# A batched matrix product whose engines run on hand-written semaphores, with one buffer of transposes, one of rounded y and three of x

## The chip, the cores and the metric

The kernel runs on one core of a Trainium2 chip. The metric is the device time of one execution in microseconds (us): 134.47 us before the change, the median of three executions (134.36 to 134.61). The profile covers one execution, from its first instruction to its last, which is a little shorter than the device time: its span is 132.9 us.

Five engines take part. TensorE (PE in the profile) multiplies, VectorE (DVE) and ScalarE (ACT) copy and convert, SyncE (SP) only issues DMA transfers, which sixteen DMA engines then carry out. GpSimd (POOL) does nothing but set up four constants.

## The reference

```python
batch, dim_i, dim_j, dim_k = 32, 256, 512, 384
# x: (32, 256, 512) float32, y: (32, 512, 384) float32
np.einsum('bij,bjk->bik', x, y).astype(np.float32)
```

So there are 32 independent products of a 256 x 512 and a 512 x 384 matrix. Both kernels round x and y to 16-bit floating point for the multiplication and accumulate in 32 bits.

## The kernel before

The batch is worked off in N = 8 iterations of four matrices each (Q = 4). Each of the four occupies 32 of the 128 partitions. An iteration n consists of these parts, and letters stand for them:

- x, y: the loads of 2.1 MB of x and 3.1 MB of y, both issued by SyncE.
- T: VectorE rounds x to 16 bits (one cast, 128 x 4096) and transposes it in two halves, e = 0 and e = 1.
- R: VectorE rounds y to 16 bits in four casts, a quarter each.
- M: TensorE makes 128 products, 64 for each half e. Each uses 32 rows of the array, and four matrices g take turns.
- C and D: ScalarE (C) and VectorE (D) copy the eight PSUM banks, one for each (e, g), into the output tile. A bank is copied in four pieces of 32 partitions, from iteration 6 on in two pieces of 64.
- S: the store of 1.6 MB, issued by SyncE on the same queue as the loads.

The order in which a scheduler keeps them is written down in a plan. Every engine works off its own parts in this order, and the framework places the semaphores from the tiles that the instructions read and write.

```python
PLAN = """
x0 x1 y0
T0 x2 y1
T1 R0 M0 C0 x3 y2
T2 D0 R1 M1 C1 x4 y3
T3 D1 R2 M2 C2 x5 y4
T4 D2 R3 M3 C3 x6 y5
T5 D3 R4 M4 C4 x7 S0 S1 S2 y6
T6 D4 R5 M5 C5 y7
T7 D5 R6 M6 C6 R7 M7 C7 D7 S3 S4 S5 S6 S7
"""
...
    x_pool = ctx.enter_context(tc.tile_pool(name="x_pool", bufs=2))
    y_pool = ctx.enter_context(tc.tile_pool(name="y_pool", bufs=2))
    xr_pool = ctx.enter_context(tc.tile_pool(name="xr_pool", bufs=1))
    xt_pool = ctx.enter_context(tc.tile_pool(name="xt_pool", bufs=3))
    yr_pool = ctx.enter_context(tc.tile_pool(name="yr_pool", bufs=2))
    o_pool = ctx.enter_context(tc.tile_pool(name="o_pool", bufs=O_BUFS))
...
    def on_vector(n, e, g):
        if n < WIDE_GROUPS:                       # WIDE_GROUPS = 6
            return (e, g) == (NE - 1, Q - 1)
        return n == N - 1 and g % 2 == 1
...
    def multiply(n):
        ...
        for e in range(NE):
            for g in range(Q):
                ps_of[n, e, g] = bank[e, g]
            for t in range(T):
                for g in range(Q):
                    s = slice(g * PQ, (g + 1) * PQ)
                    keep(nc.tensor.matmul(ps_of[n, e, g], xt[s, e, t // 2, :, t % 2],
                                          y_r[s, t], start=(t == 0), stop=(t == T - 1)))
```

So half e of M needs four PSUM banks at once, which C and D of the iteration before must have emptied; there is one set of eight banks.

## Time and profile before

| what | before |
|---|---|
| device time | 134.47 us (134.36 to 134.61) |
| span of the profiled execution | 132.9 us |
| mean granted TensorE clock | 0.848 |
| busy: PE, VectorE, ScalarE | 61.5, 96.1, 91.7 us |
| moved by DMA | 54.68 MB, mean 412 GB/s |
| HBM read, written | 41.94 MB, 12.58 MB |
| one cast of x | 2.29 us (8 of them) |
| one transpose, 128 x 1024, and 128 x 512 | 2.00 us (12), 1.08 us (8) |
| one cast of a quarter of y | 0.953 us (32) |
| one copy out of PSUM, ScalarE and VectorE | 0.471 us (192), 0.556 us (32) |
| SyncE's waits before y loads, for VectorE's cast of y | 29.8 us |
| SyncE's waits before stores, for ScalarE's copies | 24.4 us |

How to read it: busy time is how long an engine executed instructions; a wait is put down to whatever ended it. The slices in the profile cut the span into 40 equal pieces of 3.3 us each, and a digit is the busy share in tenths. Where lines of a timeline are shown, the first two numbers are start and length in us, and the bracket at the end tells how long the engine sat idle before the first of these instructions and what released it. L followed by a number is a line of the kernel; a q behind an engine's name stands for its sequencer, which for SyncE is the one that issues DMA. The landing of a transfer is when its last part is reported as complete.

### The profile page before, as it was taken

Reading aid. Unit: us, or ns where it says so; the run is one execution under the profiler, and the core shown is the slowest. Engines: PE = TensorE matmul, PEld = TensorE weight load, DVE = VectorE, ACT = ScalarE, POOL = GpSimd, SP = SyncE. Lnnn points to the kernel's source line nnn. Section 1 sums busy time; section 2 is a strip of 40 time slices with the busy share of each in tenths; the row PEclk is TensorE's granted clock in tenths of the full one; section 3 lists DMA queues with packets and bytes.
Section 4 is the critical chain, followed back from the end, with each engine's and each line's share of the span. In section 5 each row is a group of like instructions: output and inputs, shape, how many; then the busy total and the mean of one; then the engine's idle time right before and its main releaser. Section 6 shows DMA issues by size and latency. Waiting matters only on the chain.

```text
span 132.9 us, 2437 instructions
## 1 busy us (share of the span) xinstructions
PE 61.5 (46%) x1024; PEld 34.9 (26%) x1024; DVE 96.1 (72%) x92; ACT 91.7 (69%) x193; POOL 0.2 (0%) x4
## 2 busy tenths in 40 slices
PE   0000004990399129924952395329540079887100
PEld 0000002550147014612541153115320034455000
DVE  0049999699959999999997999699951090735600
ACT  3000000089999999999999999999999961998500
POOL 0000000000000000000000000000000000000000
PEclk9999999999658975797799869985999555999955
DMA  4999999999999999999999999999999999999993
GB/s 109 429 424 441 451 414 429 446 429 412 419 471 407 404 437 441 432 409 446 429 417 414 456 432 402 414 419 429 429 464 429 414 451 400 419 425 412 400 412 141
DMA packets 3723, 54.68 MB, mean 412 GB/s; under 512 B 384, under 2 KB 384, under 8 KB 896
## 3 DMA queue, kind: packets, MB, share of 16 engines
q1 hardware_dynamic: 3712, 54.53, 96.9%
q8 instruction: 8, 0.13, 0.4%
q14 instruction: 3, 0.02, 0.0%
HBM read 41.94 MB, written 12.58 MB: 410 GB/s over the span
## 4 chain that ended last, share of the span: by engine, by line
DMA 45%; DVE 19%; ACT 15%; PE 10%; issue 4%; DVEq 1%
DMA x_sb<-in_x_dram 22%; DMA y_sb<-in_y_dram 22%; ACT o_sb L153 15%; PE o_ps L132 10%; DVE xt_sb L113 6%; DVE x_r L106 5%; DVE o_sb L153 4%; DVE y_r L119 4%; DVEq L202 1%; DVEq L106 0%
## 5 line engine op out<-in xcount | busy, mean ns | idle before, releaser
L153 ACT COPY o_sb<-o_ps 32x384 f32<-32x384 f32 (+1 forms) x192 | 90.4, 471 | 32.7 <-PE o_ps L132 25.8
L132 PE MATMUL o_ps<-y_r,xt_sb 32*128 32x384 f16 x1024 | 61.5, 399 | 61.7 <-DVE y_r L119 52.3
L132 PEld LDWEIGHTS <-xt_sb 32*128 32x128 f16 x1024 | 34.9, 113 | 87.9 <-DVE y_r L119 32.8
L119 DVE CAST y_r<-y_sb 128x1536 f16<-128x1536 f32 x32 | 28.5, 953 | 10.3 <-DMA y_sb<-in_y_dram 10.2
L113 DVE STREAM_TRANSPOSE xt_sb<-x_r 128x1024 f32<-128x1024 f32 (+1 forms) x20 | 31.7, 1631 | 0.3
L106 DVE CAST x_r<-x_sb 128x4096 f16<-128x4096 f32 x8 | 18.3, 2292 | 11.1 <-DMA x_sb<-in_x_dram 11.0
L153 DVE COPY o_sb<-o_ps 32x384 f32<-32x384 f32 (+1 forms) x32 | 17.8, 556 | 7.8 <-PE o_ps L132 3.8
L153 ACT ACT_TABLE_LOAD x1 | 1.3, 1283 | 0.7 <-PEq L191 0.7
L191 POOL MEMSET const-uint8-127<- 128x1 uint8 x1 | 0.1, 103 | 0.0
L191 POOL MEMSET const-bfloat16-1.0<- 128x1 bf16 x1 | 0.1, 102 | 0.0
L191 POOL MEMSET const-float32-0.0<- 128x1 f32 x1 | 0.1, 99 | 0.2 <-issue 0.2
L191 POOL MEMSET const-float32-1.0<- 128x1 f32 x1 | 0.1, 99 | 0.0
## 6 DMA issues: line engine op xcount, KB each, us to landing
y_sb<-in_y_dram SPq DMA_DIRECT2D x8, 3072.0 KB, 21.5
x_sb<-in_x_dram SPq DMA_DIRECT2D x8, 2048.0 KB, 22.0
out_dram<-o_sb SPq DMA_DIRECT2D x8, 1536.0 KB, 25.6
```

The costliest lines, as they stand in the source:

```text
L106: keep(nc.vector.tensor_copy(x_r, x_of.pop(n)))
L113: keep(nc.vector.transpose(dst[:, c, e], src[:, c, e]))
L119: keep(nc.vector.tensor_copy(yr_of[n][:, a : a + STEP], y_sb[:, a : a + STEP]))
L132: nc.tensor.matmul(ps_of[n, e, g], xt[s, e, t // 2, :, t % 2], y_r[s, t], start=(t == 0), stop=(t == T - 1),)
L153: keep(copy(o[a : a + w, g // per, h * NE + e], ps[h * w : (h + 1) * w]))
L191: nc = _bacc.Bacc("TRN2", target_bir_lowering=False, num_devices=1)
L202: with _tile.TileContext(nc) as tc:
```

## The change

All engines' instructions are put into one section in which the framework places no semaphore and changes no order. Each engine gets its own list of work, and the kernel allocates and waits on its own semaphores. The purpose is a form in which TensorE's code could be written as a loop over iterations (the switch for that, `LOOP`, is off here, so the products are written out as before). A loop needs its operands at the same addresses in each turn, which is why there is a single buffer of rounded y and a single buffer of transposes for iterations 0 to 6; iteration 7 has a buffer of transposes of its own. The memory that this frees is partly given to a third buffer of x.

The core of the diff (cuts marked by "..."):

```diff
-PLAN = """ ... """
+X_BUFS = 3
+Y_BUFS = 2
+LOOPED = 7
+LOOP = False
+QUEUE = "x0 x1 y0 x2 y1 x3 y2 x4 y3 x5 y4 x6 y5 x7 S0 S1 S2 y6 y7 S3 S4 S5 S6 S7"
+
+VECTOR = """
+X0 T0 R0 X1 T1 R1 X2 D0 T2 R2 X3 D1 T3 R3 X4 D2 T4 R4 X5 D3 T5 R5 X6 D4 T6
+X7 T7 D5 R6 D6 R7 D7
+"""
...
-    x_pool = ... bufs=2      y_pool = ... bufs=2     xr_pool = ... bufs=1
-    xt_pool = ... bufs=3     yr_pool = ... bufs=2    o_pool = ... bufs=O_BUFS
+    x_all = pool.tile([P, X_BUFS, R, J], F32, name="x_sb")
+    y_all = pool.tile([P, Y_BUFS, T, K], F32, name="y_sb")
+    o_all = pool.tile([P, O_BUFS, R, K], F32, name="o_sb")
+    x_r = pool.tile([P, R, J], MM_DT, name="x_r")
+    y_r = pool.tile([P, T, K], MM_DT, name="y_r")
+    xt = [pool.tile([P, NE, TW, P], F32, name=f"xt_sb_{k}") for k in range(2)]
...
     def on_vector(n, e, g):
         if n < WIDE_GROUPS:
             return (e, g) == (NE - 1, Q - 1)
-        return n == N - 1 and g % 2 == 1
+        return g == Q - 1 and e == NE - 1 if n < N - 1 else g % 2 == 1
...
+        def load_x(n):
+            if n >= X_BUFS:
+                eng.wait_ge(x_cast, n - X_BUFS + 1)
+        def load_y(n):
+            if n >= Y_BUFS:
+                eng.wait_ge(y_ready[NA - 1], n - Y_BUFS + 1)
+        def store(n):
+            eng.wait_ge(act_done[NE - 1], n + 2)
+            eng.wait_ge(vec_done, n + 2)
...
+        def transpose_x(n):
+            ...
+            for e in range(NE):
+                if 0 < n < LOOPED:
+                    eng.wait_ge(products, done(n - 1, e, Q - 1))
+                for c in range(b):
+                    i = eng.transpose(dst[:, c, e], src[:, c, e])
+                i.then_inc(x_ready[e], 1)
+        def round_y(n):
+            eng.wait_ge(y_in[n], 16)
+            for a in range(NA):
+                if n > 0:
+                    if a < NA - 1:
+                        eng.wait_ge(y_done, (NA - 1) * (n - 1) + a + 1)
+                    else:
+                        eng.wait_ge(products, done(n - 1, NE - 1, Q - 1))
+                s = slice(a * STEP, (a + 1) * STEP)
+                eng.tensor_copy(y_r[:, s], y_all[:, n % Y_BUFS, s]).then_inc(y_ready[a], 1)
...
+        for e in range(NE):                      # TensorE, one iteration
+            eng.wait_ge(act_done[e], count)
+            if e == NE - 1:
+                eng.wait_ge(vec_done, count)
+            eng.wait_ge(x_ready[e], count)
+            for t in range(T):
+                if e == 0 and t % STEP == 0:
+                    eng.wait_ge(y_ready[t // STEP], count)
+                ... matmul as before, the last of a bank adds 1 to products ...
+                if e == NE - 1 and t % STEP == STEP - 1 and t < T - 1:
+                    i.then_inc(y_done, 1)
...
+    with tc.tile_critical():
+        queue()
+        scalar()
+        vector()
+        tensor()
```

In the string VECTOR, X stands for the cast of x alone and T for the two halves of the transpose; the other letters are as above. VectorE works it off from left to right. Iteration 6's bank (1, 3) is now VectorE's to copy (D6), so ScalarE has two copies fewer.

## The prediction

> **What bounds the kernel now.** I read the 40 slices first, then the DMA queues, then each engine in order of time.

> ```profile
> DVE  0049999699959999999997999699951090735600
> ACT  3000000089999999999999999999999961998500
> PEclk9999999999658975797799869985999555999955
> DMA  4999999999999999999999999999999999999993
> q1 hardware_dynamic: 3712, 54.53, 96.9%
> ```

> Only the DMA row is full from the second slice to the last but one: the one queue works 96.9% of the span. 54.53 MB are moved; the stretches of 4 us between 4 and 124 us show 397 to 451 GB/s. So the kernel is bound by bytes, and the end is set by when the last bytes are queued. That is in the stretches of 1 us near the end (columns: PE, PEld, DVE, ACT, POOL busy, PEclk, DMA share, GB/s) and in the queue's last issue:

> ```profile
> 129.00:130.00 1.00, 0.00 (x0) 0.00 (x0) 0.00 (x0) 0.00 (x0) 0.00 (x0) 0.50 1.03 430
> 130.00:131.00 1.00, 0.00 (x0) 0.00 (x0) 0.00 (x0) 0.00 (x0) 0.00 (x0) 0.50 0.61 252
> ```

> ```profile
> 125.58 0.38 SPq L160 DMA_DIRECT2D out_dram<-o_sb  x1
> ```

> (and, over the eight stores:)

> ```profile
> DMA to landing us min/median/max: 6.5/25.6/31.0
> ```

> The DMA engines run dry at about 130.6 us. The last store S7 is issued at 125.58 and lands after 6.5 us (the minimum of the eight stores), at 132.1; 0.8 us later the span ends. S7 is 1.57 MB, at 420 GB/s 3.7 us of transfer, so S6 in front of it ends at about 130.6 - 3.7 = 126.9. **The slack of S7's issue is therefore about 126.9 - 125.6 = 1.3 us**, less the time a store needs to get going. A change that issues S7 earlier gains almost nothing; one that issues it over a microsecond later pays.

> What leads to S7 is in the timelines of ACT, PE and VectorE (start, us, engine, line, idle before it and its releaser):

> ```profile
> 27.09 81.51 ACT L153 COPY o_sb<-o_ps 32x384 f32<-32x384 f32 x168 [25.08 <-PE o_ps L132]
> 112.60 9.80 ACT L153 COPY o_sb<-o_ps 64x384 f32<-64x384 f32 x20 [4.00 <-issue]
> ```

> ```profile
> 89.25 4.30 PE L132 MATMUL o_ps<-y_r,xt_sb 32*128 32x384 f16 x63 [1.28 <-ACT o_sb L153]
> 95.07 2.78 PE L132 MATMUL o_ps<-y_r,xt_sb 32*128 32x384 f16 x62 [1.52 <-ACT o_sb L153]
> 107.23 8.67 PE L132 MATMUL o_ps<-y_r,xt_sb 32*128 32x384 f16 x131 [9.38 <-DVE y_r L119]
> ```

> ```profile
> 90.10 2.29 DVE L106 CAST x_r<-x_sb 128x4096 f16<-128x4096 f32 x1
> 92.42 4.06 DVE L113 STREAM_TRANSPOSE xt_sb<-x_r 128x512 f32<-128x512 f32 x4
> 97.95 2.26 DVE L153 COPY o_sb<-o_ps 32x384 f32<-32x384 f32 x4 [1.47 <-ACT o_sb L153]
> 106.21 3.56 DVE L119 CAST y_r<-y_sb 128x1536 f16<-128x1536 f32 x4 [5.99 <-DMA y_sb<-in_y_dram]
> 113.71 3.56 DVE L119 CAST y_r<-y_sb 128x1536 f16<-128x1536 f32 x4 [3.94 <-DMA y_sb<-in_y_dram]
> ```

> I write X, T, R, M, C, D for rounding x, transposing, rounding y, products, ScalarE's and VectorE's copies of an iteration, a and b for the two halves (e = 0, 1). **ScalarE is the second limit**: 168 copies (C0 to C5) without a pause, 81.51 / 168 = 0.485 us each, 28 per iteration, 13.59 us. So C_n ends at 27.09 + 13.59 (n + 1): C3 at 81.4, C4 at 95.0 (PE's half b of M5 starts at 95.07, when C4 has freed its banks), C5 at 108.6. VectorE's work per iteration is X 2.29 + T 3.95 + D 2.27 + R 3.57 = 12.1 us, less than that; with two y_r and three xt it runs ahead and has slack at the end: before R6 it waited 5.99 us for y6, before R7 3.94 us for y7.

> [...] M6's first half of 64 took 107.23 to 112.60, 5.4 us (84 ns each), the second about 2.8 us (43 ns); M5's first half, which warmed up on its way, 4.30 us.

> **The change, part by part.**

> 1. *Work.* The same 1024 products, 20 transposes, 40 casts, 24 transfers of the same shapes and nearly the same order; two copies of iteration 6 go from ScalarE to VectorE. Nothing is taken off the DMA engines. Own semaphores replace equally many waits. The section adds a branch in and out and a joint wait; the barriers of before take 0.73 us at the start and 0.8 us at the end, so I allow +0.2 us.

> 2. *Third x buffer.* x2 is issued at about 2 us instead of 10.73. But x0, x1, y0 (7.3 MB) keep the queue busy until about 20 us anyway. Gain 0.

> 3. *R0 before X1.* y0 lands about 20.6 (1.65 plus the shortest y landing, 18.9), and R0 ran at 20.81. M0, and with it the chain of ScalarE, starts 0.2 us earlier.

> 4. *One y_r, one xt for iterations 0 to 6.* T_n's half b must wait for M_(n-1)b, R_n's last quarter for the same, and M_(n-1)b waits for C_(n-2). So VectorE is tied to ScalarE. From C_(n-2)'s end: M_(n-1)b 2.8, T_n b 2.0, R_n 3.6, X 2.3, D 2.3, T_(n+1) a 2.0 = 15.0 us; then T_(n+1) b waits until 13.6 + 2.8 = 16.4. It fits: the period stays 13.59 us, with 1.4 us of slack per turn. ScalarE goes on without pauses, since M_n a starts 7.8 us into C_(n-1) and takes 4.3 to 5.4 of the remaining 5.8 us.
>    The loads: R_n ends at (end of C_(n-2)) + 8.4, R4 at 76.2, R5 at 89.8; before they ended at 76.6 and 90.2. So y6 and y7 are issued as before and the queue stays full.

> 5. *The end, where the tie costs.* T6's half b waits for M5b, which starts with the end of C4 at 95.0 and ends at 97.9. Only then come, in this order, T6b 2.05, X7 2.30, T7 4.07, D5 2.27 and R6, with 0.1 of gaps: 97.9 + 10.8 = **R6 at 108.7 instead of 106.21, +2.5 us**. Before, X7 and T7 ran at 90.10 to 96.5, ahead of M5b. Then:
>    - M6a starts a quarter of R6 (0.95) later, 109.7, and is cold: 4.4 to 5.4 us, to 114.6 (before 112.6); M6b 2.8, to 117.4.
>    - D6 now stands ahead of R7 and waits for all of M6: 2 x 0.56 = 1.1, to 118.7. R7 118.7 to 122.3 (before 113.71 to 117.27): **+5 us**. Of this M7 did not use all: before it was held by C6 on ScalarE, 112.60 + 16 copies, until 120.5 for half b. Now C6 is 14 copies from 114.6, done at 121.4.
>    - M7a ends 0.7 after R7, 123.0; M7b 2.8, 125.8 (before 120.50 + 2.75 = 123.25); D7's last four 2.3, 128.1. **S7 at 128.2 instead of 125.58, +2.6 us.**
>    - S6 is queued at about 121.5, in time. The engines run dry at 126.9, and S7 pays its own start: 128.2 + about 6.2 (a little under the 6.5 of before, which held 1.3 us of queue, but a start of its own: x0 took 8.41 - 0.73 = 7.7 us for 2.1 MB, that is 5.0 of transfer and 2.7 of start and landing; 3.7 + 2.5 = 6.2) = 134.4 instead of 132.1, **+2.3 us**.

> Sum: +2.3 (tail) + 0.2 (section) - 0.2 (R0) = +2.3 us; 134.47 + 2.3 = 136.8.

> **Rivals.** (a) *The transfers hide it all*: DMA is full and bytes are the same, so 134.5 to 135. For it: 96.9%. Against: S7's slack of 1.3 us is smaller than the 2.6 us above; it needs M6a warm early and no wait in D6. (b) *ScalarE starves*: if M_n a takes 5.4 us cold and half b is late each turn, ScalarE pauses every iteration, say 0.5 us over five, so +2.5 more at the tail: 139. For it: the margin is 0.4 us when cold. Against: M3 to M5 took 4.3 us. (c) *The loads run late*, since y_(n+2) waits for R_n which waits for products: the queue would empty near 62 or 75 us. Against: R2 ends at 49 and R3 at 63, 12 us ahead of need. (d) *The third x buffer and less waiting gain*: under 134. Nothing in a full DMA row leaves room; I give it 3 in 100.

> **Range and chances.** The tail's sum has about 1 us of doubt from the clock of M6a and M7a, 0.7 from the start of S7, and rival (a) below and (b) above: 135.0 to 138.8. The 2% line is 137.16, close above my number: slower 0.40, within 0.57, faster 0.03.

> **What would show it.** Right: R6 starts near 108.7 without waiting for DMA; T6's second half is released by PE at about 97.9; R7 is released by VectorE's copies or PE, not by y7; S7 is issued near 128; the DMA row has a dip in the slice before the last; the row of ScalarE stays full from 27 to 108. Wrong: S7 issued before 126.5 (then 134.5), a DMA gap in mid-span, pauses in ScalarE's copies, or matmuls of another length than 43 and 84 ns.

## The result, and the profile after

The changed kernel takes 141.59 us (median of four executions, 141.18 to 142.35) where the kernel before takes 134.42 in the same series: 1.054 times as long, with a 95% interval of 1.049 to 1.059. The prediction said 136.8 us and at most 138.8. Its executions also spread far more: six further ones of the unaltered kernel, on another chip, lay between 137.13 and 146.05 us, while the kernel before stayed between 134.27 and 134.71 beside them. The experiments trace the first fact to its cause and the second in part. Below, medians are compared; an interval given with a ratio leaves out executions far above the fastest, so in kernels that spread it can lie below the ratio of the medians.

The page of the changed kernel, in 40 slices of 3.5 us, and its load and store queue:

```profile
DVE  0049309981997599889957997999489992393900
ACT  3000000499999994999999989999999401983700
PEclk9999999995595955995959559868685556977975
DMA  4999999999999999999999999999999999939264
q1 hardware_dynamic: 3712, 54.53, 92.6%
```

The same packets and bytes as before, but the DMA row, full from the second slice to the 35th, has holes in the last five. So mid-span lost nothing on the queue: the difference shows at the end alone. The stretches of 1 us there (PE, PEld, DVE, ACT, POOL busy, clock, DMA share, GB/s) show the holes:

```profile
123.00:124.00 1.00, 0.92 (x20) 0.51 (x24) 1.00 (x2) 0.98 (x3) 0.00 (x0) 0.99 0.32 135
124.00:125.00 1.00, 1.00 (x16) 0.50 (x12) 1.00 (x2) 0.88 (x2) 0.00 (x0) 0.50 0.00 0
```

The queue runs dry twice, from 123.8 to 125.8 us and from 130.4 to 133.4, because S6 and S7 come late. SyncE's issues of S6 and of S7 (start, length in us):

```profile
124.92 0.39 SPq L122 DMA_DIRECT2D out_dram<-o_sb  x1
```

```profile
132.67 0.38 SPq L122 DMA_DIRECT2D out_dram<-o_sb  x1
```

S6 is issued at 124.9 (before: 120.5) and S7 at 132.7 (before: 125.6), 7.1 us later. With nothing ahead of it in the queue S7 lands after 5.2 us instead of 6.5, at 137.9 instead of 132.1, 5.8 us later. The span of the profiled execution grew by 6.5 us (132.9 to 139.4), the median time by 7.2. Why S6 and S7 are late is in two timelines. TensorE, one line per half M_a or M_b of an iteration, with the idle time before it in the bracket:

```profile
42.39 4.27 PE L215 MATMUL o_ps<-y_r,xt_sb 32*128 32x384 f16 x64 [2.68 <-issue]
49.78 5.31 PE L215 MATMUL o_ps<-y_r,xt_sb 32*128 32x384 f16 x64 [3.12 <-DVE y_r L190]
56.84 2.78 PE L215 MATMUL o_ps<-y_r,xt_sb 32*128 32x384 f16 x64 [1.75 <-issue]
62.85 4.28 PE L215 MATMUL o_ps<-y_r,xt_sb 32*128 32x384 f16 x64 [3.23 <-ACT o_sb L144]
69.79 4.22 PE L215 MATMUL o_ps<-y_r,xt_sb 32*128 32x384 f16 x64 [2.67 <-issue]
...
97.16 4.20 PE L215 MATMUL o_ps<-y_r,xt_sb 32*128 32x384 f16 x64 [2.70 <-issue]
```

And VectorE over one turn, X3, D1, T3 in its two halves and R3, and later T6b, R6 and D6:

```profile
52.17 2.28 DVE L165 CAST x_r<-x_sb 128x4096 f16<-128x4096 f32 x1
54.48 2.26 DVE L144 COPY o_sb<-o_ps 32x384 f32<-32x384 f32 x4
56.77 2.06 DVE L178 STREAM_TRANSPOSE xt_sb<-x_r 128x1024 f32<-128x1024 f32 x1
59.74 2.01 DVE L178 STREAM_TRANSPOSE xt_sb<-x_r 128x1024 f32<-128x1024 f32 x1 [0.91 <-PE o_ps L215]
61.67 3.53 DVE L190 CAST y_r<-y_sb 128x1536 f16<-128x1536 f32 x4
...
101.47 2.08 DVE L178 STREAM_TRANSPOSE xt_sb<-x_r 128x512 f32<-128x512 f32 x2 [2.29 <-PE o_ps L215]
...
112.34 3.57 DVE L190 CAST y_r<-y_sb 128x1536 f16<-128x1536 f32 x4
120.81 1.13 DVE L144 COPY o_sb<-o_ps 64x384 f32<-64x384 f32 x2 [4.91 <-PE o_ps L215]
```

The reader is to lay the two side by side. D1 ends at 54.48 + 2.26 = 56.74, and M2b starts at 56.84. D2 ends at 69.70 (in the timeline's next turn, 67.43 + 2.27), and M3b starts at 69.79. Every M_b starts 0.1 us after VectorE's copy of the iteration before, although the profile calls the wait "issue" and names nobody. M_b in turn releases the second half of the next transposes: M2b ends at 59.62, T3b starts at 59.74. Then R, X and D follow on VectorE, and with D the next M_b. **This is a closed loop of two engines**: M_b 2.78 + T_b 2.01 + R 3.5 + X 2.3 + D 2.3 = 12.9 us. From the end of D1 to that of D2 it took 12.96 us. Where M_b takes 4.2 us instead, the loop takes 14.4: D2 to D3 (84.10) is such a turn. From M1b (42.39) to M5b (97.16) four turns take 54.8 us, two of 14.4 and two of 12.96. That is 13.7 on average, a little above ScalarE's 13.5, and 2.9 us more than four fast turns would take.

The long halves are TensorE's slow clock: 66 ns per product on average over the half instead of 43, with a mean granted clock of 0.64 in M1b and 0.65 in M3b and M5b, and of 1.00 in M2b and M4b. In this trace M_b is fast after a gap of 1.75 us and slow after one of 2.7. VectorE's late copy sets when M_b starts, 6.9 to 7.1 us after M_a in each of these turns; the gap is what M_a, itself fast or slow, leaves of that. How the clock follows is shown under experiment 3.

### The profile page after: what moved, and what is told of

Same layout as the page of the kernel before. It is cut to its first block, busy times and chain, and to the rows that moved or that the text cites. A ratio compares the mean times of both kernels' runs of the same rounds, so it can differ in the third digit from the quotient of the medians.

```text
span 139.4 us, 2469 instructions
## 1 busy us (share of the span) xinstructions
PE 62.9 (45%) x1024; PEld 34.7 (25%) x1024; DVE 97.1 (70%) x94; ACT 90.7 (65%) x191; POOL 0.2 (0%) x4
## 3 DMA queue, kind: packets, MB, share of 16 engines
q1 hardware_dynamic: 3712, 54.53, 92.6%
## 4 chain that ended last, share of the span: by engine, by line
PE 34%; ACT 25%; DMA 14%; DVE 12%; issue 9%; SPq 1%; DVEq 0%
PE o_ps L215 34%; ACT o_sb L144 25%; DMA y_sb<-in_y_dram 14%; DVE xt_sb L178 4%; DVE o_sb L144 4%; DVE y_r L190 3%; DVE x_r L165 2%; SPq L107 1%; SPq L267 0%; DVEq L141 0%; DVEq L186 0%; DVEq L164 0%; SPq L237 0%
## 5 line engine op out<-in xcount | busy, mean ns | idle before, releaser
L144 ACT COPY o_sb<-o_ps 32x384 f32<-32x384 f32 (+1 forms) x190 | 89.5, 471 | 40.4 <-PE o_ps L215 38.1
L215 PE MATMUL o_ps<-y_r,xt_sb 32*128 32x384 f16 x1024 | 62.9, 415 | 67.3 <-DVE y_r L190 49.3
L215 PEld LDWEIGHTS o_ps<-y_r,xt_sb 32*128 32x128 f16 x1024 | 34.7, 117 | 95.2 <-issue 65.9
L178 DVE STREAM_TRANSPOSE xt_sb<-x_r 128x1024 f32<-128x1024 f32 (+1 forms) x20 | 32.4, 1642 | 9.4 <-PE o_ps L215 9.1
L144 DVE COPY o_sb<-o_ps 32x384 f32<-32x384 f32 (+1 forms) x34 | 18.9, 556 | 8.0 <-PE o_ps L215 7.4
```

The source lines that it names most:

```text
L144: i = copy(o[a : a + w, g // per, h * NE + e], bank[e, g][h * w : (h + 1) * w])
L178: i = eng.transpose(dst[:, c, e], src[:, c, e])
L215: i = eng.matmul(bank[e, g], w[s, e, t // 2, :, t % 2], y_r[s, t], start=(t == 0), stop=(t == T - 1),)
```

## The experiments

Names: X, T, R, D, M, C, S as in the prediction. In each edit only what differs from the changed kernel is shown.

**1. VectorE's copy placed earlier** (label d_early), nothing else changed:

```diff
-X0 T0 R0 X1 T1 R1 X2 D0 T2 R2 X3 D1 T3 R3 X4 D2 T4 R4 X5 D3 T5 R5 X6 D4 T6
-X7 T7 D5 R6 D6 R7 D7
+X0 T0 R0 X1 T1 D0 R1 X2 T2 D1 R2 X3 T3 D2 R3 X4 T4 D3 R4 X5 T5 D4 R5 X6 T6
+D5 X7 T7 R6 D6 R7 D7
```

> VectorE copies its bank of iteration n-1 directly behind the transposes of n, ahead of rounding y of n (in the changed kernel it does so two steps later, behind the next cast of x). Buffers are as in the changed kernel. Theory 1 (VectorE's late copy holds the second half of the products, and through the single buffer of transposes this closes a loop between VectorE and TensorE of 12.96 us warm and 14.4 us cold): the second halves start when ScalarE has emptied its banks and take 2.8 us each, ScalarE copies without a pause from 26.3 us on, R6 starts near 108, S7 is issued near 128, time 136 to 137.5. Theory 2 (the single buffers alone tie VectorE to ScalarE and this costs the time): R6 stays near 112, time stays 141 to 142. Theory 3 (what costs is TensorE's clock, cold by the shape of the single section): second halves stay 4.2 us every other iteration, 140 to 142.

Measured: 137.05 us (136.06 to 138.20), 1.016 times before (1.010 to 1.023). ScalarE's, TensorE's and VectorE's timelines of this kernel:

```profile
26.83 67.74 ACT L144 COPY o_sb<-o_ps 32x384 f32<-32x384 f32 x140 [24.44 <-PE o_ps L215]
94.73 13.50 ACT L144 COPY o_sb<-o_ps 32x384 f32<-32x384 f32 x28 [0.16 <-PE o_ps L215]
```

```profile
89.38 8.02 PE L215 MATMUL o_ps<-y_r,xt_sb 32*128 32x384 f16 x128 [5.57 <-DVE y_r L190]
```

```profile
108.21 3.53 DVE L190 CAST y_r<-y_sb 128x1536 f16<-128x1536 f32 x4
```

ScalarE copies from 26.83 to 108.23 us with one pause of 0.16 us, M5 is one run without a gap between its halves and ends at 97.40 (changed kernel: 101.36), R6 starts at 108.2, S7 is issued at 128.24. Another order of the same work in the same buffers gives back 4.7 of 7.2 us (2.4 us above the kernel before in the same series). This is theory 1; the two others expected no change.

**2. Three numbers of buffers, one at a time.** Transposes used in turn in the two buffers that were there already (xt2):

```diff
-dst = xt[n // LOOPED] ...       wait for products of n - 1, if 0 < n < LOOPED
+dst = xt[n % 2] ...             wait for products of n - 2, if n > 1
```

> Only the two existing buffers of transposes are used in turn (n modulo 2), so that the transposes of n wait for the products of n-2; order, single buffer of rounded y and three x buffers as in the changed kernel. Theory 1: the loop between VectorE and TensorE is cut, VectorE runs on at 12.1 us per iteration as the loads allow, X7 and T7 come before 97 us, R6 starts at the landing of y6 (106.4), S7 is issued near 126, time 134.5 to 135.5. Theory 2 in its form that the single rounded y ties VectorE to the products: R waits instead, time 137 to 140. Theory 3: 140 to 142.

Two buffers of rounded y (yr2), with the waits on n - 2 likewise:

```diff
-y_r = pool.tile([P, T, K], MM_DT, name="y_r")
+y_rs = [pool.tile([P, T, K], MM_DT, name=f"y_r_{k}") for k in range(2)]
```

> Two buffers of rounded y, everything else as in the changed kernel (one buffer of transposes for iterations 0 to 6). Theory 1: the loop runs through the transposes and not through rounded y, so its period stays 13.7 us and only R7 at the end no longer needs the products of iteration 6 (it stands behind D6 all the same): 140.5 to 142. Theory 2: a part of the loss returns, 137 to 139.

Two x buffers (x2):

```diff
-X_BUFS = 3
+X_BUFS = 2
```

> Two x buffers instead of three, everything else as in the changed kernel. All theories that see the loads in mid-span as hidden: the queue stays full until about 122 us, time 141.6, within 0.7. If the third buffer gains something that the rest of the change hides: 143 or more.

Measured: xt2 135.40 us (135.38 to 135.44), 1.007 times before (1.005 to 1.009); yr2 141.68 (140.85 to 144.07); x2 141.62 (139.87 to 143.98). The single buffer of transposes is one link of the loop, and cutting it is enough even with the copy left late. TensorE's M1b and VectorE's R6 in xt2:

```profile
42.59 4.46 PE L215 MATMUL o_ps<-y_r,xt_sb 32*128 32x384 f16 x64 [2.25 <-issue]
106.27 3.57 DVE L190 CAST y_r<-y_sb 128x1536 f16<-128x1536 f32 x4 [2.15 <-DMA y_sb<-in_y_dram]
```

A slow half still occurs, but where no loop closes over it the time does not show it. R6 waits for the landing of y6 again, as X7 and T7 no longer stand behind M5b: xt2 cuts the loop and the tie at the end together, so it does not part the two. The single buffer of rounded y is not a link of the loop, and doubling it alone leaves the median where it was. Nor does the third x buffer show in the medians, though kernels that spread by 3 to 4 us would hide a gain of some tenths. In x2 the queue was not full throughout, against what was expected (289 to 363 GB/s in three slices between 79 and 90 us), but the end is set by VectorE and TensorE and not by the loads.

**3. The slow clock's share.** Sixteen further products, each repeating the first contraction step and then overwritten, go ahead of each M_a (warm16); then the same in iterations 0 to 5 alone (warm16_mid), since in warm16 they also lengthened M6 and M7 at the tail:

```diff
-for t in range(T):
+for k, t in enumerate([0] * EXTRA[e] + list(range(T))):      # EXTRA = (4, 0)
...
-    start=(t == 0), stop=(t == T - 1)
+    start=(t == 0), stop=(t == T - 1 or k < EXTRA[e])
```

> The changed kernel with 16 additional products ahead of each iteration's first half, each a repetition of the first contraction step that is then overwritten (128 more products in all, outputs as before). They fill a part of the idle time between the two halves. If the slow clock in every other second half (4.2 us instead of 2.8) is a part of the loss, all second halves take 2.8 us, the loop's period falls from 13.7 to about 13.5 us where ScalarE limits it, M5's second half starts near 94.5 instead of 97.16 and ends near 97.3 instead of 101.36, S7 is issued 3 to 4 us earlier, time 137 to 139, in spite of 12% more products. If the clock plays no part, 141.5 to 143.

> As warm16, but with the 16 additional products in iterations 0 to 5 alone: in warm16 they also lengthened M6 and M7 at the tail (M6 took 8.10 us instead of 7.18, M7 7.71 instead of 7.19), which hid a part of what the warm clock gave back. If every other second half's 1.4 us of slow clock is a part of the loss: all second halves of iterations 1 to 5 take 2.8 us, M5 ends near 97.2 instead of 101.4, time 137.5 to 139.5. If it plays no part: the same as the changed kernel, 141 to 142.5.

Beside warm16_mid the unaltered changed kernel ran again:

> The changed kernel unaltered, on the same chip as warm16_mid, since its executions spread by more than a microsecond[...]: 141 to 142.5.

Measured: warm16 140.28 us (138.49 to 141.14), less of a gain than expected. warm16_mid 138.33 (138.08 to 139.81), against 142.11 (137.13 to 146.05) of the unaltered kernel on the same chip. Of that one the spread was not expected. TensorE in warm16_mid, iteration 2:

```profile
48.52 5.11 PE L216 MATMUL o_ps<-y_r,xt_sb 32*128 32x384 f16 x80 [3.39 <-ACT o_sb L145]
55.31 2.78 PE L216 MATMUL o_ps<-y_r,xt_sb 32*128 32x384 f16 x64 [1.68 <-issue]
```

With 96 products more, the median is 3.8 us lower (3.2 by the distance from the kernel before, if the first four executions of the changed kernel are taken), although one execution of the unaltered kernel took only 137.13. The extra work fills a part of the gap, the second halves take 2.78 us wherever the trace separates them, and the loop's 12.96 us stay below ScalarE's 13.5. So the late copy costs most of what it costs by way of the clock: **it leaves TensorE idle, the array slows, the slow half (4.2 us instead of 2.78) lengthens the loop that contains it**.

```profile
38.65:42.05 3.40, 1.07 (x28) 0.47 (x19) 3.33 (x5) 3.31 (x8) 0.00 (x0) 1.00 1.03 441
42.05:45.45 3.40, 3.06 (x40) 1.81 (x44) 2.27 (x2) 3.32 (x8) 0.00 (x0) 0.50 0.94 402
52.30:55.70 3.40, 2.79 (x36) 1.26 (x28) 3.34 (x4) 1.57 (x5) 0.00 (x0) 0.50 1.04 448
55.70:59.10 3.40, 2.26 (x56) 1.70 (x60) 3.08 (x3) 3.32 (x8) 0.00 (x0) 1.00 0.95 405
```

```profile
38.40:41.80 3.40, 1.90 (x48) 1.04 (x40) 3.34 (x4) 3.26 (x8) 0.00 (x0) 1.00 1.01 434
41.80:45.20 3.40, 2.70 (x64) 1.82 (x64) 2.62 (x3) 3.32 (x8) 0.00 (x0) 1.00 0.98 410
```

M1b is slow because the clock fell to 0.50 after a stretch with 1.07 us of products, and M2b is fast because it rose to 1.00 after one with 2.79. In warm16 the extra products make the first figure 1.90, the clock stays, and M1b takes 2.78 us after a gap of 2.20. In the traces of the kernels before and after, between 20 and 120 us, the stretches after which a clock of 1.00 fell had at most 1.26 us of busy PE, those after which it stayed at least 1.82; those after which a clock of 0.50 stayed had at most 2.52, those after which it rose at least 2.79. What lies between these figures the two traces do not show. The length of a gap alone does not decide: in the second trace of the unaltered kernel a gap of 2.07 us was followed by a slow half (4.46 us).

This bears on the spread. In the two traces of the unaltered kernel the instants lie differently against its start: in the second one they are 43.55, 46.95, 50.35, and the slow second halves are M1b, M2b and M4b instead of M1b, M3b and M5b. The spread fell from 8.9 us to 1.7 with the extra products. That this phase makes the whole spread is not shown, as the fastest and the slowest execution left no trace.

**4. The order at the tail.** R7 ahead of D6, in the changed kernel (r7_d6: "... D5 R6 R7 D6 D7"):

> The changed kernel with only the last two of VectorE's tasks in another order: R7 ahead of D6 (rounding y of iteration 7 no longer waits behind the copy of iteration 6's bank, which waits for all of M6). R7 can start on the quarters of rounded y as M6's second half frees them, near 118.8 instead of 121.97; M7's second half then waits for ScalarE's C6 until 124.9. If the order at the tail costs what the profile suggests: S7 issued near 130.2 instead of 132.7, 138.5 to 139.7. If the whole loss comes from mid-span: 141 to 142.

Measured: 138.39 us, from 135.67 to 140.56 in four executions, with no interval; in a kernel that spreads by itself this decides nothing. The same question was put again in a steadier kernel, below.

**5. Is it the section itself?** Own semaphores, but the buffers, the order and the banks of the kernel before (section_before):

```diff
+VECTOR = "X0 T0 X1 T1 R0 X2 T2 D0 R1 X3 T3 D1 R2 ... X6 T6 D4 R5 X7 T7 D5 R6 R7 D7"
+three buffers of transposes, two of rounded y, X_BUFS = 2
+iteration 6 wholly on ScalarE
```

> Own semaphores and one section as in the changed kernel, but with the buffers of the kernel before (two of x, three of transposes, two of rounded y), VectorE's order of before, and iteration 6's banks all on ScalarE as before. If the section and its semaphores by themselves cost only their entry and exit: 134.9 to 135.4. If they cost anything in the stream of instructions: 137 or more.

Measured: 135.33 us (135.16 to 135.63), 1.008 times before (1.006 to 1.009): 1.0 us. The span is 0.6 us longer, 133.5. The first transfer is issued at 0.93 instead of 0.73 us. S7, issued at 125.87 and landing after 6.1 us (the stores' minimum), is complete at 132.0, and the span goes on for 1.5 us more, where it was 0.8 before. So in this execution the cost lies at the entry and the exit, and the stream between them runs as before.

**6. A repair that keeps the single buffers in the part that is to be looped** (own67): the copy early, transposes of iterations 6 and 7 in buffers of their own, R7 ahead of D6; then with the loop switched on (own67_loop), and with D6 ahead of R7 again (own67_d6):

```diff
-LOOPED = 7
+LOOPED = 6
-dst = xt[n // LOOPED] ...       # two buffers
+dst = xt[max(0, n - LOOPED + 1)] ...   # three buffers
+... T5 D4 R5 X6 T6 X7 T7 D5 R6 R7 D6 D7
```

> A repair that keeps one buffer of transposes for iterations 0 to 5 and one of rounded y: the copy D of n-1 directly behind the transposes of n, buffers of transposes of their own for iterations 6 and 7, R7 ahead of D6. By theory 1, with the tail's order: R6 near the landing of y6 (106.4 to 107), S7 issued near 125, time 134.7 to 135.5. If single buffers cost of themselves: 137 or more.

> The repair own67 with TensorE's code for iterations 0 to 5 written as a loop, which is what the single buffers are for. Fewer instructions have to be fetched for TensorE (768 pairs' worth of code less: 640 products with their weight loads), so less instruction traffic on the DMA engines that carry the loads; in the kernels without the loop y1 lands about 1.5 us later than the steady pace of the other loads. If that lag is the fetching of instructions: up to 1.5 us less than own67, 133.9 to 135.0. If the fetches cost nothing: 135.3 to 135.7. If the loop's turn holds TensorE, 136 or more.

> The repair own67 with D6 ahead of R7 again, as in the changed kernel: the tail's order alone, in a kernel whose time varies little. R7 then waits for all of M6 (near 115.5) and D6, instead of running from the landing of y7 at 113.7; M7 moves by about 2 to 3 us and S7 is issued near 127.5 instead of 125: after the queue has run dry, so 136 to 137.5. If the tail's order is hidden behind the queue: 135.2 to 135.7.

Measured: own67 135.46 us (135.15 to 135.62), 1.008 times before (1.006 to 1.010), equal to section_before; R6 starts at 107.24, R7 at the landing of y7. So one buffer of rounded y, and one of transposes for iterations 0 to 5, cost nothing that shows in this order. own67_loop 135.55 (135.34 to 136.21): TensorE's code becomes shorter by 640 products and their weight loads, and the queue that fetches instructions shows it, first in own67, then in own67_loop (packets, MB, share of 16 engines):

```profile
q8 instruction: 8, 0.13, 0.4%
```

```profile
q8 instruction: 3, 0.05, 0.1%
```

But the time stays. The DMA row is full to the end anyway, and 0.08 MB are nothing beside 54.5. The expectation that a lag of y1 comes from these fetches fell; its cause is open. own67_d6 135.92 (135.28 to 137.04): the tail's order is worth 0.4 to 0.5 us at the median, less than expected. In its trace S7 is issued at 126.35 instead of 125.00 and lands after 5.6 instead of 7.1 us, so the later issue is hidden in the queue, and the spans are 133.5 and 133.6. No version here beats the kernel before.

## Why the prediction was wrong

**The bound and the slack: right.** The end is set by when S7 reaches the queue, and beyond some 1.3 us it pays in full. In own67_d6 S7 came 1.35 us later than in own67 and landed no later; in the changed kernel it came 7.1 us later than in the kernel before and landed 5.8 us later, which leaves the 1.3. The queue stayed full in mid-span and the work was unchanged, as forecast. So the rivals (a), (c) and (d), a hidden change, late loads and a gain, fell. That a full queue can move no more was the author's estimate; the trace of the kernel before shows a mean of 428 GB/s between 4 and 124 us, and single stretches of 4 us from 397 to 451.

**The section and the start (steps 1 and 3): too small.** The allowance of 0.2 us for the section measured 1.0. The 0.2 us by which M0 was to start earlier did not come: it starts at 22.07 instead of 21.78, as the first load is issued 0.2 us later.

**The tie (step 4): here it failed.** The prediction let M_(n-1)b wait "for C_(n-2)" alone, and closed with "It fits". In the kernel M_b waits for `act_done` **and** for `vec_done`. D_(n-2), moved behind R_(n-1) and X_n in the new order, is the later of the two. The sum of 15.0 us even contained D's 2.3, as VectorE's work, but not as something that M_b must wait for. So it was laid out as a chain with 1.4 us of slack per turn, where it is a loop of 12.96 or 14.4 us. It also took M_b at 2.8 us throughout. Nothing in the kernel before had shown a second half after an idle gap of 2.7 us (its gaps were about 1.6, and the halves after them took 2.78). Instead of starting with C4's end at 95.0, M5b started at 97.16 and took 4.20: 101.36 instead of 97.9. The pauses in ScalarE that rival (b) named did occur (1.80 and 0.34 us), so that rival was right in part: M2a was cold (5.31 us), and as the loop had made it start late, at 49.78, it ended 1.8 us after C1.

**The tail (step 5): right in form, from a wrong start.** T6b, X7, T7, D5 after M5b took 10.9 us, 101.47 to 112.34, where 10.8 were predicted. With the copy early, where step 4's assumption holds, the numbers came out nearly as written: R6 at 108.2 (108.7), S7 at 128.24 (128.2), 137.05 us (136.8). The prediction was thus one of d_early. That the time fits to 0.3 us is in part luck: the section cost 0.8 us more than allowed, and S7's landing took 1.0 us less. In the changed kernel R6 came 3.6 us after the forecast, and S7 4.5: M7 took 7.19 us, with a first half slower than reckoned, and D7 waited for it. Two terms of the tail were mis-sized besides: S6 was not "in time" (124.9, the queue dry since 123.8), and S7, with no queue in front of it, landed after 5.2 us, not 6.2.

**What remains of the 7.2 us.** The medians lie above that of the kernel before in the same series by 7.2 us in the changed kernel, 2.4 in d_early and 1.1 in own67. So 4.7 come from the late copy with the loop it closes (changed kernel to d_early), 1.3 from X7 and T7 behind M5b and the tail's order (d_early to own67), and 1.1 remain, about what the section cost in section_before (1.0). Of the 4.7, the slow clock is the larger part (3.2 to 3.8 in warm16_mid), but the two are not separate sums, as warm halves make the loop shorter than ScalarE's pace. One overlooked wait is thus the difference between a forecast that is 0.3 us off and one that is 4.8 us off.

## What to carry to other kernels

When buffers become single and order is written by hand, write down for every wait of one engine all engines that release it, and follow each back until it ends in a load or comes round to itself: a path that comes round is a loop whose period is the sum of its members, and it needs neither a busy engine nor an empty queue to become the bound. Put a copy that another engine waits for directly behind the work that it needs, not behind the next piece of input. And look behind a wait that leaves TensorE idle for what it costs in the work that follows: here the same 64 products took 4.2 us instead of 2.78 after gaps of 2.7 us, and filling a part of the gaps gave back 3.2 to 3.8 of the 4.7 us that the late copy cost.

## What the runs showed of the hardware that was not expected

In the changed kernel the same 64 products took 2.78 us after a gap of 1.75 us and 4.2 after one of 2.7; what went with it, in the traces of the kernels before and after, was how long PE had been busy in the 3.41 us stretch before (at most 1.26 us: a clock of 1.00 fell to 0.50; at least 1.82: it stayed). Adding 96 products whose results are thrown away lowered a kernel's median by 3.8 us. And one unaltered kernel, alone on one core, ran between 137.13 and 146.05 us in six executions, while section_before and xt2, in which that loop is cut, stayed within 0.5 us in four executions each.
